# Encoder block on one core: two kinds of head pairs taken in turn, token loads first, statistics a block ahead

## The chip, the cores and the metric

The kernel runs on one core of one Trainium2 chip. The metric is the device time of one execution in microseconds. Three runs of the kernel before took 2289.86 to 2292.59 us, median 2290.41 us.

## The reference

One layer of a bidirectional encoder, run on two requests with the same weights: a prompt of 512 tokens and a sample of 1024 tokens, model width 1024.

```
h = rmsnorm(x);  proj = h @ w_in          # q, k, v of 8 heads A, q, k, v of 12 heads B, gates gA, gB
A: 2-D neighbourhood attention on rows of 64 tokens, window min(8, rows) x 16, bias rpb[head, dy, dx]
B: 3 groups of 4 heads, dilations 1, 4, 16; each query sees 64 keys on either side at its dilation,
   bias from a table of 32 buckets; the 3 groups are combined by their softmax denominators
merged = sigmoid(gA) * (oA @ wA) + sigmoid(gB) * (oB @ wB);   x = x + merged @ w_out
x = x + relu(rmsnorm(x) @ w_up)^2 @ w_down
```

All of it is float32 in the reference. q and k are normalised per head before the scores.

## The kernel before, in words

Both requests stand one behind the other as 1536 tokens, in three blocks b of 512 (block 0 is the prompt). Every large product is made of three fp16 matmuls on the high and low halves of both operands (`mm3`, lines 168 to 171); a weight is scaled by its own norm before it is halved.

**Stages.** First the tokens are normalised: `stats` (791) adds the squares of a block into `acc` and makes `rmsr`, the inverse norm of each token along the free axis, by way of two small matmuls (`ssx` 805, `bcx` 814) and a power on POOL (`rc` 810). `build` (782) multiplies the tokens by it (785, every third on POOL) and writes the halves `act` (hi 786 on ACT, lo 787 on DVE). Then come four gate column tiles g0 to g3 for the three blocks (`gate_mm`, 24 matmuls of 512 columns a block), then ten pairs of heads. Pairs 0 to 5 are dilated (B, two times the three dilations), pairs 6 to 9 are 2-D (A). A pair projects four token tiles of the prompt (names with `0b` or `0a`) and eight of the sample (`1b`, `1a`), 24 matmuls of 384 columns a tile (`pj0b`, `pj1a`...). One gate tile (g4 to g10) follows each of pairs 0 to 6, and five more (g11 to g15) follow pair 9. After that come the branch product, the output product and the MLP, from about 1015 us on.

**Attention** runs beside the projection of the pair behind it. `run` (680) advances by steps, a step being half a token tile of projection; the attention of a pair begins 8 steps after its last tile (LAG) and takes one unit every two steps: scores (`s`, `t`, 449), softmax, halves of the probabilities (`p`), a transposing DMA (`pT`, 470), and two units later the products with the values (`o`, 481 and 482). The normalised q and k are transposed by a DMA as well (`qk`, 382); v goes through memory (`v_d`, loaded as `v0b`, `v1a`...). A pairs load a bias of 256 KB (`ba0a`) or 768 KB (`ba1a`) three times a pair and a request; when the three groups of half of the B heads are done, `combine` (608) loads their outputs (`G`) and writes the combined ones. `branch_bound` (306) loads a weight in 18 pieces (`bn`) for its norm.

**Weights** (lines 71 to 122) stream through ten float32 slots (`st_g`, `st_p`) and fifteen fp16 slots (`w_g`, `w_p`). Each `tick` splits one piece, makes the scale of a tile that has all its squares (`scale_of`, with a small matmul `fro_g` or `fro_p`, 189, that stands in PE's queue), squares one piece and issues one load.

**Tables.** `tables` (688) builds the biases of both kinds in memory by DMAs from memory to memory: `vec_d`, `tb_d` (two of 768 KB), `tc_d` (two of 256 KB), 24 `r_d` of 30 KB, then `ct`, `c_d` and 21 pieces of `ba_d`. `b0b` and `b1b` load the B biases from them.

**What sets the order.** The program is written in the order that the Python code issues it, and buffers are recycled through pools; each engine works through its own queue in order. All DMAs but two are issued by SP, so the SP queue is one list in which a DMA that waits for its data holds every later one.

## Time and profile before

| | |
|---|---|
| median of 3 runs | 2290.41 us |
| the profiled execution's own time | 2283.75 us |
| its span, first to last instruction | 2282.0 us |
| mean granted clock of TensorE, of full speed | 0.976 |
| busy: PE, DVE, ACT, POOL | 2134.1, 1244.4, 993.5, 302.0 us |
| mean busy share of the 16 DMA engines, moved | 45% of the span for SP's queue, 259.10 MB |

PE is busy 94% of the span. The page's 40 slices (57 us each) show PE at 9 tenths or more in nearly all of them; the exceptions are the first four slices and those from the 12th to the 17th. The mean over the span says little about a stage, so the rows below cut it by stages: the start (0 to 96 us is blocks 0 and 1 of the gates, to 124 block 2), the B pairs from there to about 640, the A pairs to about 960, the last gates to 1040.

### The profile page before, as it was taken

The numbers are of one execution on the slowest core, as the hardware profiler recorded it, in microseconds if no ns is written. First come the engines' busy times: TensorE is split into PE (matmuls) and PEld (weight loads), VectorE is DVE, ScalarE is ACT, GpSimd is POOL, SyncE is SP. The second block draws the span as 40 slices with busy tenths as digits, with TensorE's granted clock in tenths as the row PEclk, the third lists the DMA queues.
The fourth block names the chain that finished last, engine by engine and source line by source line (L and its number), as shares of the span: only waits on it lengthen the run. The fifth ranks groups of instructions, "written<-read, shape, count | busy, mean of one in ns | idle before, by whom it ended". The sixth has DMA issues, their size and how long they took to land.

```text
span 2282.0 us, 32442 instructions
## 1 busy us (share of the span) xinstructions
PE 2134.1 (94%) x11440; PEld 1089.6 (48%) x11440; DVE 1244.4 (55%) x3245; ACT 993.5 (44%) x2432; POOL 302.0 (13%) x434
## 2 busy tenths in 40 slices
PE   5778999999997876989999999999999999999999
PEld 2334565556554544544444544444444444444444
DVE  6534766686567766646734544444444444444444
ACT  5234656566545664537633523233333333222222
POOL 1112322232223423100000000000000000000000
PEclk9888999999999998999999999999999999999999
DMA  5249886676669999878531110111111111111102
GB/s 165 77 140 264 196 178 156 156 175 144 142 135 188 189 186 184 173 177 283 191 130 37 56 32 28 52 56 56 56 56 56 56 56 56 39 38 36 37 1 111
DMA packets 372908, 259.10 MB, mean 114 GB/s; under 512 B 241152, under 2 KB 333184, under 8 KB 372744
## 3 DMA queue, kind: packets, MB, share of 16 engines
q1 hardware_dynamic: 372598, 257.01, 45.0%
q8 instruction: 90, 1.47, 0.3%
q14 instruction: 74, 0.61, 0.1%
q10 hardware_dynamic: 146, 0.01, 0.0%
HBM read 164.02 MB, written 53.29 MB: 95 GB/s over the span
## 4 chain that ended last, share of the span: by engine, by line
PE 71%; DMA 12%; DVE 5%; SPq 2%; ACT 2%; issue 1%; POOL 1%; ACTq 0%; DVEq 0%; POOLq 0%
PE up L169 7%; PE dn L169 7%; PE dn L170 7%; PE up L170 7%; PE dn L171 7%; PE up L171 7%; PE g L169 2%; PE g L170 2%; PE g L171 2%; PE pj1b L169 2%; PE pj1b L171 2%; PE pj1b L170 2%; PE op L169 2%; PE op L171 2%; PE op L170 2%; DMA pT1a<-p1a 2%
## 5 line engine op out<-in xcount | busy, mean ns | idle before, releaser
L948 DVE SCALAR_TENSOR_TENSOR y<-dn,und,y 128x512 f32<-128x512 f32 x384 | 287.0, 750 | 180.9 <-PE dn L171 180.6
L1126 ACT ACTIVATE r<-up,alpha 128x512 f32<-128x512 f32 x96 | 65.3, 680 | 592.2 <-PE up L171 592.1
L169 PE MATMUL up<-xp,w_u 128*128 128x512 f16 x768 | 291.0, 379 | 1.0 <-ACT xp L1049 1.0
L171 PE MATMUL dn<-w_d,u 128*128 128x512 f16 x768 | 291.1, 379 | 0.0
L171 PE MATMUL up<-xp,w_u 128*128 128x512 f16 x768 | 291.0, 379 | 0.0
L170 PE MATMUL dn<-w_d,u 128*128 128x512 f16 x768 | 291.0, 379 | 0.0
L170 PE MATMUL up<-xp,w_u 128*128 128x512 f16 x768 | 291.0, 379 | 0.0
L169 PE MATMUL dn<-w_d,u 128*128 128x512 f16 x768 | 291.0, 379 | 0.0
L1130 DVE TENSOR_TENSOR u<-r,u 128x512 f16<-128x512 f32 x96 | 66.3, 692 | 284.2 <-ACT u L1129 280.4
L169 PE MATMUL g<-act,w_g 128*128 128x512 f16 x384 | 148.3, 393 | 14.1 <-ACT act L786 14.1
L170 PE MATMUL g<-act,w_g 128*128 128x512 f16 x384 | 149.0, 388 | 6.1 <-DVE act L787 6.0
L171 PE MATMUL g<-act,w_g 128*128 128x512 f16 x384 | 148.8, 388 | 0.0
L169 PE MATMUL pj1b<-w_p,act 128*128 128x384 f16 x384 | 126.6, 330 | 2.4 <-DVE o1b L451 2.4
L171 PEld LDWEIGHTS <-act 128*128 128x128 f16 x960 | 95.6, 100 | 66.1 <-issue 6.9
L169 PEld LDWEIGHTS <-act 128*128 128x128 f16 x960 | 98.2, 102 | 60.0 <-issue 6.4
L170 PEld LDWEIGHTS <-act 128*128 128x128 f16 x960 | 96.5, 100 | 63.2 <-issue 11.3
L171 PE MATMUL pj1b<-w_p,act 128*128 128x384 f16 x384 | 126.1, 328 | 0.0
L170 PE MATMUL pj1b<-w_p,act 128*128 128x384 f16 x384 | 126.1, 328 | 0.0
L169 PEld LDWEIGHTS <-u 128*128 128x128 f16 x768 | 76.3, 99 | 89.0
L169 PEld LDWEIGHTS <-w_u 128*128 128x128 f16 x768 | 76.4, 100 | 88.5
L171 PEld LDWEIGHTS <-u 128*128 128x128 f16 x768 | 75.1, 98 | 90.6
L171 PEld LDWEIGHTS <-w_u 128*128 128x128 f16 x768 | 75.1, 98 | 90.5
(330 smaller groups left out, 4233.3 us busy)
## 6 DMA issues: line engine op xcount, KB each, us to landing
st_n<-in_wn SPq DMA_DIRECT2D x32, 512.0 KB
st_u<-in_wu SPq DMA_DIRECT2D x32, 512.0 KB
st_d<-in_wd SPq DMA_DIRECT2D x32, 512.0 KB
st_p<-in_wp SPq DMA_DIRECT2D x80, 192.0 KB
z_d<-z SPq DMA_DIRECT2D x48, 256.0 KB
z<-z_d SPq DMA_DIRECT2D x48, 256.0 KB
ba1a<-ba_d SPq DMA_DIRECT2D x12, 768.0 KB
st_g<-in_wg SPq DMA_DIRECT2D x32, 192.0 KB
```

Source lines behind the costliest of these rows:

```text
L169: nc.tensor.matmul(ps, ah, bh, start=first, stop=False)
L170: nc.tensor.matmul(ps, ah, bl, start=False, stop=False)
L171: nc.tensor.matmul(ps, al, bh, start=False, stop=last)
L948: nc.vector.scalar_tensor_tensor(out=out, in0=ps, scalar=scale, in1=out, op0=ALU.mult, op1=ALU.add)
L1126: nc.scalar.activation(s, ps[b], AF.Relu, scale=alpha[:, f:f + 1])
L1130: nc.vector.tensor_tensor(out=uu[:, 1, i, tb], in0=s, in1=uu[:, 0, i, tb], op=ALU.subtract)
```

## The change

1. ORDER and AFTER: the pairs are taken in the order B0 B1 B2 A6 B3 A7 B4 A8 B5 A9. Of the seven gate tiles between pairs, one stands behind pair 0 and two behind each of A6, A7 and A8. The first A pair waits until all tables have been issued, and the attention's generator doesn't end before the last combine.
2. `past`: a weight load is issued, and a piece squared early, by the count of splits of two ticks ago rather than the present one.
3. Start: tokens of block 0 are loaded ahead of most weights, those of blocks 1 and 2 right behind nine weight pieces. All squares of the tokens are made on ACT; their adds are made on DVE for block 0 and on POOL for blocks 1 and 2. The statistics of block b+1 are begun in the middle of block b, and three of its builds stand ahead of the fourth gate tile of block b. The steps of the tables begin in block 2.
4. The last steps of `ba_d` come every three steps of the background rather than every four.

```diff
+ORDER = (0, 1, 2, 6, 3, 7, 4, 8, 5, 9)
+AFTER = (1, 0, 0, 2, 0, 2, 0, 2, 0, 0)
...
-        while n and self.nload < min(len(self.units), self.nsplit + RAW):
+        while n and self.nload < min(len(self.units), self.past[0] + RAW):
...
-                                      or self.nload == self.nsplit + RAW):
+                                      or self.nload == self.past[0] + RAW):
...
+        self.past = [self.past[1], self.nsplit]
...
-    for i in range(10):
+    between, c = {}, NFIRST
+    for i, n in zip(ORDER, AFTER):
         W.add(("p", i), [(wp[i, k], 384) for k in range(KT)])
-        if i < NBETWEEN:
-            add_gate(NFIRST + i)
+        between[i] = range(c, c + n)
+        for c in between[i]:
+            add_gate(c)
+        c = between[i].stop
+    assert c == 16 - NFILL
...
-            for i, kind in enumerate(kinds):
+            for i in ORDER:
+                kind = kinds[i]
...
-                    if i < NBETWEEN:
-                        c = NFIRST + i
+                    for c in between[i]:
...
         def attn_a(self, p):
+            for _ in tab:
+                pass
...
+            while not self.combined:
+                yield
...
+            self.combined = True
...
-                for _ in range(4 if col else 2):
+                for _ in range(3 if col else 2):
...
-                src = xch[b][k]
-                if k == 0:
-                    nc.gpsimd.tensor_tensor(out=acc, in0=src, in1=src, op=ALU.mult)
-                else:
-                    sq = pp.tile([P, 512], F32, tag="p16", bufs=2, name=f"sqx{b}_{k}")
-                    nc.scalar.activation(sq, src, AF.Square)
-                    nc.vector.tensor_tensor(out=acc, in0=acc, in1=sq, op=ALU.add)
+                sq = pp.tile([P, 512], F32, tag="p16", bufs=2, name=f"sqx{b}_{k}") if k else acc
+                nc.scalar.activation(sq, xch[b][k], AF.Square)
+                if k:
+                    (nc.gpsimd if b else nc.vector).tensor_tensor(out=acc, in0=acc, in1=sq, op=ALU.add)
...
-            nc.gpsimd.tensor_tensor(out=rc, in0=rs, in1=mhalf, op=ALU.pow)
+            rsqrt(rc, rs)
...
         ld = load_x(0)
-        ps = [psum(f"g{c}_0") for c in range(3)]
-        W.load(3)
         for k in range(KT):
             next(ld)
-            if k % 2:
-                W.load(1)
+            if k == 3:
+                W.load(3)
+        W.load(6)
         gain()
         st = stats(0)
         next(st)
-        for _ in range(4):
-            W.tick(2)
-        next(st)
-        for _ in range(3):
-            W.tick(2)
-        next(st)
-        with tc.issue_after(xch["w"]):
-            for _ in load_x(1):
+        for b in (1, 2):
+            for _ in load_x(b):
                 pass
-        for k in range(KT):
-            build(0, k)
-            if k == 0:
-                W.ahead(("g", 2), 0)
-            for c in range(3):
-                gate_mm(c, 0, ps[c], k)
-        for c in range(3):
-            gate_out(c, 0, ps[c])
-        norms()
...
-        tab = tables(pp)
+        for _ in range(5):
+            W.tick(0)
         next(st)
         next(st)
-        for k in range(KT):
-            build(1, k)
+        norms()
+        tab = tables(pp)
+        ahead = 0
+        for b in range(NB):
+            ps = [psum(f"g{c}_{b}") for c in range(3)]
+            for k in range(KT):
+                if k >= ahead:
+                    build(b, k)
+                if b == 0 and k < 7:
+                    W.tick(0)
+                for c in range(3):
+                    gate_mm(c, b, ps[c], k)
+                if b == 2:
+                    next(tab)
+                if k == 4 and b < 2:
+                    st = stats(b + 1)
+                    next(st)
+            if b < 2:
+                next(st)
             for c in range(3):
-                if k == 0:
-                    ps[c] = psum(f"g{c}_1")
-                gate_mm(c, 1, ps[c], k)
-        for c in range(3):
-            gate_out(c, 1, ps[c])
-        st = stats(2)
-        next(st)
-        for c in range(3, NFIRST):
-            gate_step(c, 1)
-            next(tab)
-        next(st)
-        next(st)
-        for k in range(KT):
-            build(2, k)
-            for c in range(3):
-                if k == 0:
-                    ps[c] = psum(f"g{c}_2")
-                gate_mm(c, 2, ps[c], k)
-            next(tab, None)
-        for c in range(3):
-            gate_out(c, 2, ps[c])
+                gate_out(c, b, ps[c])
+            if b < 2:
+                next(st)
+                ahead = 3
+                for k in range(ahead):
+                    build(b + 1, k)
+            for c in range(3, NFIRST):
+                gate_step(c, b)
+                W.tick()
+                W.tick()
+        for c in range(NFIRST):
             W.release(("g", c))
             W.tick()
+            W.tick()
         tab = behind(tab)
-        for c in range(3, NFIRST):
-            gate_step(c, 2)
-            W.release(("g", c))
-            W.tick()
-            next(tab)
         at = Attention(pp)
         fill = gates(16 - NFILL, 16 - NLAST)
```

Three places show what this moves. The first is DVE's queue in the start, from the token norms to the first low halves (`rmsr` is the inverse norm, `w_g` a split gate weight, `xt` the tokens of block 0, `act` their halves, `acc` the sum of squares of block 1). Before:

```order
33 L817 COPY rmsr_261<-bcx_256 128x512
34 L258 SCALAR_TENSOR_TENSOR w_g_0_277<-st_g_0_144,scales,w_g_0_277 128x384
35 L190 TENSOR_REDUCE scales<-fro_g_294 128x1
36 L258 SCALAR_TENSOR_TENSOR w_g_1_284<-st_g_1_148,scales,w_g_1_284 128x384
37 L258 SCALAR_TENSOR_TENSOR w_g_2_291<-st_g_2_152,scales,w_g_2_291 128x256
38 L785 TENSOR_TENSOR xt_139<-xt_139,rmsr_261 128x512 x4
39 L785 TENSOR_TENSOR xt_6_140<-xt_6_140,rmsr_261 128x512
40 L785 TENSOR_TENSOR xt_7_141<-xt_7_141,rmsr_261 128x512
41 L801 TENSOR_TENSOR acc_450<-acc_450,sqx_5_464 128x512
42 L191 TENSOR_SCALAR scales<-scales 128x1
43 L787 SCALAR_TENSOR_TENSOR act_112<-xt_139,nvt,act_112 128x512 x4
```

And now:

```order
24 L827 COPY rmsr_256<-bcx_251 128x512
25 L798 TENSOR_TENSOR xt_130<-xt_130,rmsr_256 128x512 x4
26 L798 TENSOR_TENSOR xt_6_131<-xt_6_131,rmsr_256 128x512
27 L798 TENSOR_TENSOR xt_7_132<-xt_7_132,rmsr_256 128x512
28 L800 SCALAR_TENSOR_TENSOR act_112<-xt_130,nvt,act_112 128x512
29 L195 TENSOR_REDUCE scales<-fro_g_286 128x1
30 L800 SCALAR_TENSOR_TENSOR act_112<-xt_130,nvt,act_112 128x512 x3
```

The three weight splits and the add for block 1 (`acc_450`) no longer stand between the norms and the first low half.

The second place is the SP queue around the first tables (`tb_d`, `tc_d` tables of the B pairs, `st_g4_2` the last third of the weights of gate tile 4, `st_p1` pieces of pair 1, `b0b0` the bias of pair 0). Before:

```order
54 L711 DMA tb_d0_78<-vec_d_77 512x1x384
55 L707 DMA vec_d_77<-vec1_804 12x512
56 L707 DMA vec_d_77<-vec2_821 12x512
57 L711 DMA tb_d1_79<-vec_d_77 512x1x384
58 L547 DMA b0b0_1492<-tb_d0_78 128x2x384
59 L714 DMA tc_d0_80<-vec_d_77 512x1x128
60 L714 DMA tc_d1_81<-vec_d_77 512x1x128
61 L547 DMA b1b0_2136<-tb_d0_78 128x2x384
62 L232 DMA st_g4_2_924<-in_wg 128x256
63 L232 DMA st_p1_0_932<-in_wp 128x384
```

And now:

```order
48 L720 DMA vec_d_77<-vec0_819 12x512
49 L720 DMA vec_d_77<-vec1_836 12x512
50 L724 DMA tb_d0_78<-vec_d_77 512x1x384
51 L724 DMA tb_d1_79<-vec_d_77 512x1x384
52 L720 DMA vec_d_77<-vec2_853 12x512
53 L237 DMA st_g4_2_920<-in_wg 128x256
54 L237 DMA st_p1_0_925<-in_wp 128x384
55 L557 DMA b0b0_1483<-tb_d0_78 128x2x384
56 L237 DMA st_p1_1_930<-in_wp 128x384
57 L237 DMA st_p1_2_935<-in_wp 128x384
58 L237 DMA st_p1_3_942<-in_wp 128x384
59 L237 DMA st_p1_4_958<-in_wp 128x384
```

Both `tb_d` now stand together and ahead of `st_g4_2`, and `tc_d` has moved behind five pieces of pair 1. In PE's queue the `fro_g` of gate tile 4, for which `st_g4_2` is squared, has moved from within the first projected tile to ahead of it.

The third place is the SP queue in the prompt's attention of pair A6, between the transposes of its third and fourth units (`pT0a6_2`, `pT0a6_3`; `ba1a6` are the biases of the sample's units, `v1a6` its values, `st_p9` and `st_g11` weights, `o_d` outputs). Before, its last twelve rows:

```order
549 L232 DMA st_p9_2_8542<-in_wp 128x384
550 L232 DMA st_p9_3_8596<-in_wp 128x384
551 L532 DMA ba1a6_1_8940<-ba_d1_92 128x2x768
552 L232 DMA st_p9_4_8636<-in_wp 128x384
553 L232 DMA st_p9_5_8668<-in_wp 128x384
554 L232 DMA st_p9_6_8714<-in_wp 128x384
555 L232 DMA st_p9_7_8746<-in_wp 128x384
556 L502 DMA v1a6_2_8944<-v_d6_71 128x1x1024
557 L232 DMA st_g11_0_8807<-in_wg 128x384
558 L502 DMA v1a6_3_9340<-v_d6_71 128x1x1024
559 L527 DMA o_d_64<-o0a6_1_0_8598 16x8x128
560 L470 DMA_TRANSPOSE pT0a6_3_0_8564<-p0a6_3_0_8561 128x8x128
```

And now, with both transposes:

```order
335 L542 DMA ba1a6_0_5276<-ba_d0_91 128x2x768
336 L512 DMA v1a6_1_5469<-v_d6_71 128x1x1024
337 L478 DMA_TRANSPOSE pT0a6_2_0_4917<-p0a6_2_0_4914 128x8x128
338 L537 DMA o_d_64<-o0a6_0_0_4950 16x8x128
339 L542 DMA ba1a6_1_5467<-ba_d1_92 128x2x768
340 L651 DMA o_d_64<-G0_2_5219 128x2x128
341 L512 DMA v1a6_2_5471<-v_d6_71 128x1x1024
342 L478 DMA_TRANSPOSE pT0a6_3_0_5013<-p0a6_3_0_5010 128x8x128
```

Before, seven weight pieces stood among them. Now the weights are elsewhere and pair A6's prompt units begin beside two gate tiles, which need no transposes of q and k.

## Rows read from the trace of the kernel before

**Rows 1.** Windows: length, busy of PE, PEld, DVE, ACT, POOL, clock, DMA share, GB/s

```profile
0.00:20.00 20.00, 3.40 (x14) 3.21 (x14) 10.06 (x25) 13.53 (x36) 3.50 (x11) 1.00 0.84 269
58.00:96.00 38.00, 25.76 (x114) 12.05 (x114) 20.60 (x28) 11.75 (x19) 7.32 (x6) 0.85 0.24 86
96.00:124.00 28.00, 27.90 (x103) 10.21 (x102) 16.25 (x31) 7.41 (x13) 2.23 (x3) 0.83 0.19 65
107.50:115.50 8.00, 8.00 (x39) 3.62 (x38) 0.95 (x4) 0.00 (x0) 0.00 (x0) 1.00 0.28 100
124.00:202.00 78.00, 55.38 (x308) 31.57 (x305) 36.49 (x117) 34.35 (x106) 18.07 (x25) 0.84 0.75 203
202.00:640.00 438.00, 431.48 (x2798) 256.76 (x2799) 282.85 (x1089) 260.58 (x872) 119.35 (x165) 0.99 0.74 168
280.00:320.00 40.00, 40.00 (x261) 23.67 (x260) 23.44 (x82) 24.25 (x86) 8.48 (x12) 1.00 0.88 197
640.00:960.00 320.00, 260.73 (x1748) 153.58 (x1747) 222.92 (x841) 182.49 (x565) 97.41 (x140) 0.93 0.92 175
960.00:1040.00 80.00, 69.55 (x415) 35.67 (x413) 38.61 (x85) 35.56 (x69) 5.53 (x13) 0.94 0.85 218
```

**Rows 2.** Waits of PE, 0 to 220 us: total us, times, longest

```profile
PE fro_g L189 <- ACT wsq L239: 18.3, 2, 9.6
PE g L169 <- ACT act L786: 14.1, 3, 6.0
...
PE g L170 <- DVE act L787: 6.0, 2, 3.2
PE bcx L814 <- POOL rc L810: 3.5, 2, 2.0
```

**Rows 3.** Timeline of the start: start us, us, engine, instructions, idle time before

```profile
19.64 1.04 POOL L797 TENSOR_TENSOR acc<-xt 128x512 f32<-128x512 f32 x1 [8.01 <-DMA xt<-in_xt]
...
20.64 1.02 POOL L810 TENSOR_TENSOR rc<-rsx,mhalf 128x4 f32<-128x4 f32 x1
...
24.87 0.61 DVE L258 SCALAR_TENSOR_TENSOR w_g<-st_g,scales,w_g 128x384 f16<-128x384 f32 x1
...
25.47 2.95 DVE L258 SCALAR_TENSOR_TENSOR w_g<-st_g,scales,w_g 128x384 f16<-128x384 f32 x2
...
28.34 3.69 DVE L785 TENSOR_TENSOR xt<-xt,rmsr 128x512 f32<-128x512 f32 x6
...
34.07 0.59 PE L170 MATMUL g<-act,w_g 128*128 128x512 f16 x1 [3.23 <-DVE act L787]
```

**Rows 4.** Timeline of DVE at block 1's builds

```profile
61.28 5.83 DVE L785 TENSOR_TENSOR xt<-xt,rmsr 128x512 f32<-128x512 f32 x6
```

**Rows 5.** Timeline of the SP queue at the tables and behind them

```profile
105.92 0.70 SPq L711 DMA_DIRECT2D tb_d<-vec_d  x1
...
119.25 8.17 SPq L714 DMA_DIRECT2D tc_d<-vec_d  x2
...
130.44 0.47 SPq L232 DMA_DIRECT2D st_g<-in_wg  x1
```

**Rows 6.** Line 721, its issues on SP: min/median/max ns, first and last

```profile
L721 SPq DMA_DIRECT2D r_d<-in_rpb x24: 802/810/1577, 20.9 to 162.0; - x24
```

**Rows 7.** Line 470, transposes of the prompt's B units on SP

```profile
L470 SPq DMA_TRANSPOSE pT0b<-p0b x24: 1188/1192/2295, 196.8 to 612.3; - x24
```

**Rows 8.** Timeline of PE at the first product with values

```profile
202.12 0.29 PE L481 MATMUL o0b<-v0b,pT0b 64*128 64x128 f16 x1 [3.33 <-DMA pT0b<-p0b]
```

**Rows 9.** Waits of PE, 640 to 1050 us: total us, times, longest

```profile
PE o1a L481 <- DMA pT1a<-p1a: 27.4, 10, 6.9
PE o0a L481 <- DMA pT0a<-p0a: 22.7, 6, 7.4
PE o1a L481 <- DVE ss1a L364: 7.1, 2, 4.2
PE s1a L449 <- DVE mn1a L451: 5.8, 1, 5.8
```

More of the change, by code (lines that the diff above doesn't have):

```diff
@@ L76, in __init__ @@
         self.nload = self.nsq = self.nscale = self.nsplit = self.free = 0
+        self.past = [0, 0]
     def add(self, key, srcs):
@@ L269, in encoder @@
         add_gate(c)
-    NBETWEEN = 16 - NFIRST - NFILL
-    for i in range(10):
+    between, c = {}, NFIRST
+    for i, n in zip(ORDER, AFTER):
         W.add(("p", i), [(wp[i, k], 384) for k in range(KT)])
-        if i < NBETWEEN:
-            add_gate(NFIRST + i)
+        between[i] = range(c, c + n)
[3 more added lines that the diff above has]
+    assert c == 16 - NFILL
     for c in range(16 - NFILL, 16):
@@ L324, in __init__ @@
         def __init__(self, pp):
-            self.pp, self.step = pp, 0
+            self.pp, self.step, self.combined = pp, 0, False
             self.pairs = []
             kinds = [dict(kind="B", g=g, jj=jj) for jj in range(2) for g in range(NG)] + [dict(kind="A")] * 4
-            for i, kind in enumerate(kinds):
+            for i in ORDER:
+                kind = kinds[i]
                 for r in range(2):
@@ L767, in gain @@
         def gain():
-            row = pp.tile([1, D], F32, tag="p16", bufs=2, name="nvrow")
+            row = pp.tile([1, D], F32, tag="G", bufs=2, name="nvrow")
             nc.scalar.dma_start(out=row, in_=nvr)
@@ L862, in encoder @@
-        norms()
-        st = stats(1)
-        next(st)
-        for c in range(3, NFIRST):
-            gate_step(c, 0)
-        with tc.issue_after(xch["w"]):
-            for _ in load_x(2):
-                pass
-        tab = tables(pp)
+        for b in (1, 2):
+            for _ in load_x(b):
+                pass
+        for _ in range(5):
+            W.tick(0)
         next(st)
         next(st)
-        for k in range(KT):
-            build(1, k)
-            for c in range(3):
-                if k == 0:
-                    ps[c] = psum(f"g{c}_1")
-                gate_mm(c, 1, ps[c], k)
@@ L879, in encoder @@
-        for c in range(3):
-            gate_out(c, 1, ps[c])
-        st = stats(2)
-        next(st)
-        for c in range(3, NFIRST):
-            gate_step(c, 1)
-            next(tab)
-        next(st)
-        next(st)
-        for k in range(KT):
-            build(2, k)
-            for c in range(3):
-                if k == 0:
-                    ps[c] = psum(f"g{c}_2")
-                gate_mm(c, 2, ps[c], k)
-            next(tab, None)
-        for c in range(3):
-            gate_out(c, 2, ps[c])
+        norms()
@@ L897, in encoder @@
+        for c in range(NFIRST):
             W.release(("g", c))
             W.tick()
+            W.tick()
         tab = behind(tab)
-        for c in range(3, NFIRST):
-            gate_step(c, 2)
-            W.release(("g", c))
-            W.tick()
-            next(tab)
         at = Attention(pp)
@@ L908, in bounds @@
         def bounds():
-            while W.nscale < W.first["p", 9] + KT:
+            while W.nscale < W.first["p", ORDER[-1]] + KT:
                 yield
```

## The prediction

> **What bounds the kernel now.** I read the windows by stage first, then the waits of PE in the stages where it is not full, then the timeline and the SP queue at those places. PE has 2134.1 of 2282.0 us of work (the page), so a change of order can win only idle time and time at the low clock (half the full one: 1.2 of 2.4 GHz). The windows show where these lie [rows 1]. From 202 to 640 us, beside the B pairs, PE is busy 431.48 of 438 us at a clock of 0.99: nothing to win. From 640 to 960 us, beside the A pairs, it is busy 260.73 of 320 at 0.93. Before 202 us it is idle or slow in every stage. After 1040 us the change moves nothing. The reader should see two separate holes: about 59 us of idle time in the A stage and a bad first fifth of a millisecond.
>
> **Start, to the end of the first gates (now 124 us).** Three steps.
>
> First, the first low half reaches PE earlier. PE's first low matmul starts at 34.07 [rows 3]. (a) Block 0's tokens have six weight pieces among and ahead of them now and three in the new order: three pieces less, 512 KB, at 269 GB/s [rows 1] 1.9 us. (b) `rc` on POOL waits for the first square of block 1, 19.64 to 20.68, while its input is there at about 19.4: 1.2 us; in the new order nothing of block 1 is on POOL there. (c) Three weight splits stand on DVE from 24.87 until the first token product at 28.34: 3.5 us, gone. (d) One add for block 1, 0.7 us as its like, between the products and the low halves, and some 0.7 us of adds ahead of the copy of `rmsr`. Sum 8.0 us.
>
> Second, the waits at the borders of the blocks. PE waits for `act` high halves 14.1 us in three places (the longest, 6.0, at block 1), for low halves 6.0 in two (the longest, 3.2, at block 0) and for `rc` 3.5 in two [rows 2]. Block 0's own (5.8, 3.2, 2.0) belong to the first step. The rest is 14.1 - 5.8 + 6.0 - 3.2 + 3.5 - 2.0 = 12.6 us. With the statistics begun in the middle of the block before and three builds ahead of the fourth gate tile, ACT, DVE and POOL do this under 72 matmuls, 15 us at the 39 in 8.00 us of [rows 1]; I leave 1.4 us, since a high half now stands behind weight squares on ACT. Gain 11.2 us.
>
> Third, the clock. Behind those waits it was low: 0.85 of 38 us and 0.83 of 28 us [rows 1] cost at most 5.7 + 4.8 = 10.5 us; part of that time PE was idle anyway, so I take 7.5. The first gates end at 124 - 26.7 = 97.3 us.
>
> What pays for it: fourteen adds move to POOL. Six token products on DVE took 3.69 us with POOL idle and 5.83 us with POOL's products beside them [rows 3, 4], so 0.36 us for each DVE instruction beside one of POOL's. Fourteen of these are 5 us of DVE time under the 15 us above, twice: on the path 0, at most 5. The Trainium skill, "SBUF — State Buffer", section "Who interferes with whom", says that a DVE instruction with two SBUF inputs contends with a GpSimd instruction that reads SBUF, the port pair being held by one at a time. It speaks against this move, and the two rows agree in sign; by the rule the cost is bounded by the adds' own time, and the sum stays as it is as long as the cover holds.
>
> **From the first gates to the first product with values (now 202.12 [rows 8]).** Two waits of PE for squares of gate weights (`fro_g`) cost 18.3 us, 8.7 and 9.6 [rows 2]. The 9.6 goes: the gate tile behind pair 1 is gone, and the next scale of a gate is due behind pair A6. The 8.7 becomes about 5: the first `tb_d` went out at 105.92, 18 us ahead of the end of the gates [rows 5]; with the steps of the tables now in block 2 I put it at about 86, 11 us ahead. A `tb_d` takes 8 us (768 KB at 100 GB/s while it runs, with a DMA share of 0.28 [rows 1]: only some of the 16 engines work for it). Both run until 102, and `st_g4_2` stands behind them, where PE at 97.3 waits for it. This piece was issued at 130.44 [rows 5]; if it doesn't wait for `tb_d`, the 5 us are a gain too. The Trainium skill, "DMA: Bandwidth & Descriptors", section "Queues, rings and completion order", says that each DMA engine takes its descriptors in ring order; by it the small load waits for the table on the shared engines, and this speaks against the two tables in a row. Without it the sum would be 5 us lower.
>
> The clock from 124 to 202 is 0.84: 12.5 us at most [rows 1], in three stretches, one behind each wait; with one gone I count 5. Two small waits ahead of the first product (0.9, and 3.3 [rows 8]) are in the chain too. PE would then be at that place at 202.1 - 26.7 - 13.3 - 5 - 4.2 = 152.9.
>
> What is late next is the SP queue, which has to reach the first `pT0b`. From 102: `tc_d` 8.2 us [rows 5], some 4 us of weights and gates, then 24 `r_d` at 0.81 [rows 6], 20 us, all of which now stand ahead of or among the first transposes; 8 transposes of q and k at 1.2 [rows 7] to 1.7, about 11; 24 small issues at 0.5 (as the `st_g` [rows 5]), 12. Sum: 102 + 8 + 4 + 20 + 11 + 12 = 157 to 158, and from the issue to PE 5.3 us (196.8 [rows 7] to 202.1): PE goes on at about 163.5, having waited 10 us. Gain of the front 38 us. Its bounds: 49 if the queue is in time, 20 if the stretch from `tb_d` to `pT0b` stays as long as it is (196.8 - 105.9 = 90.9 us, from 86: 176.9, and 5.3). I take 38, since one wait on the queue of that stretch, the one for `st_g`, is gone.
>
> **The attention stages.** Idle now: 6.5 us beside the B pairs and 59.3 beside the A pairs, and 22.4 us at most of low clock there [rows 1]; 10.4 us of the tail are not touched. In the A stage PE waits for transposed probabilities: 22.7 us for the prompt's, 27.4 for the sample's, and 12.9 for DVE (`ss1a`, `mn1a`) [rows 9]. The cause is the SP queue: the transposes stand behind biases of 768 KB, values and weights, at a DMA share of 0.92, where the B stage has 0.74. The work is the same; only its neighbours change. Mixed, the share is (438 x 0.74 + 320 x 0.92) / 715, about 0.87, and at 0.88 PE ran 40.00 of 40 us [rows 1], so the mean alone doesn't force a wait. The prompt's units of A6, A7 and A8 fall into gate tiles, and the queue between two of their transposes loses its weights: of the 22.7 us I leave 5. The sample's units run beside B projections, whose q needs no copy to `qa` on DVE: of the 27.4, 6.9 are the last unit's and stay in the tail; of the other 20.5 I leave 10. Of the 12.9, 5; 6.5 stay beside the B pairs, and 3 come new from combining and from `bn` beside A6. So 30 of 65.8 us remain: 36 gained. Of the clock I count 17 as lost now and 7 then: 10. Sum 46, taken as 45. Bounds: 0 if the DMAs set the pace wherever they stand; 83 (65.8 and 17) if all goes.
>
> **Sum.** 2283.75 - 38 - 45 = 2200.75 on the profiled execution's scale. The median of the runs lies 6.7 us above that execution, so 2207 us.
>
> **Rivals.**
> - The A stage keeps its waits, because its DMAs need the time: 2283.75 - 38 + 6.7 = 2252. For it: a share of 0.92, and biases that stand ahead of transposes in the new queue too. Against it: 0.88 with no wait at all. Chance 0.15.
> - Nearly all waits go: 2283.75 - 49 - 83 + 6.7 = 2158. For it: the gate tiles as cover; against it: `pT` still behind 768 KB. Chance 0.10.
> - Both parts give only their lower bounds, 20 and 0 (the tables' queue stays as slow, and the mix doesn't help): 2270. Chance 0.07.
> - On the other side: the A pairs' DMAs stall the B pairs too. Their idle share, 59.3 of 320 = 18.5% [rows 1], then holds over the whole mixed stage of 758 us: 140 us instead of 66, and 2283.75 - 38 + 74 + 6.7 = 2326. It decides from 13.7% idle ((66 + 38) of 758). For it: one queue for all, and B's transposes behind A's biases; against it: the low end of the share's calculation. Chance 0.07.
>
> **Numbers.** Forecast 2207 with chance 0.61, its own range 2180 to 2235. To hold 8 in 10 I reach up over the first rival and down to 2170. About 0.2%, 4.6 us, is the least that runs of this kernel tell from none. Faster 0.91 (all but the last rival and a little of the third), same 0.02, slower 0.07.
>
> **What would show it.** First low matmul near 26 us; gates over near 97 us; a wait of about 5 us at `fro_g` ahead of the first projected tile; the first product with values near 163 us behind a wait of about 10 for `pT0b`; no wait over 2 us in the prompt's units of A6 to A8; idle time of PE from there to the last gates about 30 us. It is wrong if B units (`o1b`, `o0b`) wait in the mixed stage, or if the first product comes after 180 us.

## The result, and the profile after

The changed kernel takes 2253.53 us (median of 4 runs, 2251.05 to 2257.24) against 2290.14 us for the kernel before on the same chip: ratio 0.9849, 95% interval 0.9818 to 0.988. It is faster, as forecast, but the gain is 36.6 us and not 83; 2253.53 lies near the upper end of what was held with 8 in 10 (from 2170 to over the first rival's 2252) and outside the forecast's own range (2180 to 2235).

The profiled execution took 2257.24 us, span 2255.1; with 2283.75 and 2282.0 before, the traces differ by 26.9 us. (This execution lies 3.7 us above its median and the one of before 6.4 below, so the medians differ by more.) Where the 26.9 us are shows best in three stages cut at events that both traces have: the first product with values (`o0b`), the last pair's last projection (`pj1a`), the last product of attention (`o1a`). First the windows of before at these cuts: length, busy time of PE, PEld, DVE, ACT, POOL, granted clock, DMA share, GB/s.

```profile
0.00:202.12 202.12, 139.48 (x660) 71.11 (x661) 108.79 (x257) 87.44 (x219) 38.90 (x51) 0.89 0.51 152
202.12:925.59 723.47, 659.77 (x4344) 393.69 (x4344) 484.53 (x1863) 423.02 (x1380) 211.46 (x296) 0.96 0.81 171
925.59:1013.03 87.44, 78.08 (x507) 40.81 (x506) 44.44 (x128) 43.16 (x110) 9.88 (x20) 0.98 0.85 171
```

The same of the changed kernel:

```profile
0.00:188.80 188.80, 133.10 (x659) 69.72 (x659) 108.48 (x243) 87.13 (x223) 57.67 (x62) 0.93 0.53 156
188.80:882.33 693.53, 653.24 (x4369) 391.11 (x4370) 468.31 (x1762) 412.15 (x1364) 200.69 (x290) 0.98 0.83 177
882.33:983.99 101.66, 81.61 (x482) 40.92 (x480) 59.61 (x228) 44.34 (x126) 13.90 (x25) 0.91 0.71 169
```

The front gained 13.3 us (forecast 38) and the mixed stage 29.9 (45). The last gates lost 14.2, which the prediction held untouched, and what follows lost the remaining 2. PE's idle time is the length less its busy time: 62.6 to 55.7, 63.7 to 40.3, 9.4 to 20.0 us. What is left is clock: 0.89 to 0.93, 0.96 to 0.98, but 0.98 to 0.91 beside the last gates.

The start, by the timeline (start, us, engine, what, idle time before it), answering to [rows 3]:

```profile
18.14 2.61 POOL L811 TENSOR_TENSOR acc<-acc,sqx 128x512 f32<-128x512 f32 x2 [1.03 <-ACT sqx L809]
...
20.00 8.59 DVE L798 TENSOR_TENSOR xt<-xt,rmsr 128x512 f32<-128x512 f32 x6
...
29.31 0.58 PE L175 MATMUL g<-act,w_g 128*128 128x512 f16 x1 [6.40 <-DVE act L800]
```

The six token products begin at 20.00, where before they began at 28.34, but with POOL's adds and products beside them they take 8.59 us instead of 3.69. PE's first low half comes 4.8 us earlier, not 8.

PE's waits from 0 to 220 us (total us, times, longest), to be held against [rows 2] and [rows 8]:

```profile
PE o0b L489 <- DMA pT0b<-p0b: 14.3, 1, 14.3
...
PE g L175 <- DVE act L800: 7.6, 2, 6.4
PE fro_g L194 <- ACT wsq L244: 6.4, 2, 4.9
PE fro_p L194 <- ACT wsq L244: 5.4, 1, 5.4
PE g L174 <- ACT act L799: 3.6, 2, 2.9
```

`fro_g` fell from 18.3 to 6.4 us and the waits for high halves from 14.1 to 3.6. In their place stand a wait of 5.4 us for the squares of a projection and above all 14.3 us for the first transposed probabilities. The reason is on the SP queue (start, us, what; the time of a row holds its waits), which answers to [rows 5, 7]:

```profile
93.05 3.15 SPq L724 DMA_DIRECT2D tb_d<-vec_d  x2
96.28 7.64 SPq L720 DMA_DIRECT2D vec_d<-vec  x1
104.02 0.37 SPq L237 DMA_DIRECT2D st_g<-in_wg  x1
...
118.97 6.82 SPq L295 DMA_DIRECT2D z_d<-z  x4
...
128.23 3.51 SPq L734 DMA_DIRECT2D r_d<-in_rpb  x4
...
147.35 6.77 SPq L734 DMA_DIRECT2D r_d<-in_rpb  x8
...
171.79 5.04 SPq L391 DMA_TRANSPOSE qk1b<-q161b  x1
...
184.05 1.26 SPq L478 DMA_TRANSPOSE pT0b<-p0b  x1
```

From the first `tb_d` to the first `pT0b` 91.0 us pass; before, 90.9 [rows 5, 7]. The stretch moved forward as a whole and became no shorter. The second and third rows show another cost: `st_g4_2`, for which PE waits 4.9 us, went out only after the store of the third row of bias values (`vec_d`) had held the queue for 7.64 us. From its issue to its first reader on ACT another 7.5 us passed, while the two tables were in flight:

```profile
111.50 0.42 ACT L244 ACTIVATE wsq<-st_g 128x256 f32<-128x256 f32 x1 [13.18 <-DMA st_g<-in_wg]
```

In the mixed stage, from PE's waits of 188 to 985 us (the first row has both stages, 9.9 us of it ahead of the last gates):

```profile
PE o1a L489 <- DMA pT1a<-p1a: 19.5, 9, 6.7
...
PE o1b L489 <- DMA pT1b<-p1b: 8.2, 4, 3.2
...
PE o1b L489 <- DVE vst1b L361: 4.4, 1, 4.4
...
PE o0a L489 <- DMA pT0a<-p0a: 2.8, 1, 2.8
```

Beside the last gates, PE's waits from 882 to 985 us:

```profile
PE o1a L489 <- DMA pT1a<-p1a: 9.6, 2, 6.7
PE g L174 <- ACT z L184: 5.5, 2, 4.9
PE g L174 <- DVE z L186: 3.6, 2, 3.1
```

The two rows for `z`, the eviction of a gate's sum, are new. The timelines of DVE, ACT and PE show why:

```profile
918.60 0.17 DVE L630 TENSOR_TENSOR cm<-G 128x4 f32<-128x4 f32 x1 [7.29 <-DMA G<-g_d]
...
936.31 0.52 ACT L324 ACTIVATE bn<-bn 128x384 f32<-128x384 f32 x1 [5.66 <-DMA bn<-in_wb]
936.74 0.19 ACT L324 ACTIVATION_READ_ACCUMULATOR bn<-bn 128x1 f32 x1
936.83 0.67 ACT L184 ACTIVATE z<-g,ung 128x512 f32<-128x512 f32 x1
...
937.55 0.59 PE L174 MATMUL g<-act,w_g 128*128 128x512 f16 x1 [4.92 <-ACT z L184]
```

The square of `bn` waits 5.66 us for its load, the eviction stands right behind it on ACT, and PE's next gate matmul at 937.55 has waited 4.92 us for that eviction. On DVE the combining stands so (`cm` waits 7.29 us for `G` at 918.60): in the new order both pieces of background work fall beside the last gates.

### The profile page after: what moved, and what is told of

The parts are those of the page before. It is cut to its first block, busy times and chain, and to the rows that moved or that the text cites. A ratio compares the mean times of both kernels' runs of the same rounds, so it can differ in the third digit from the quotient of the medians.

```text
span 2255.1 us, 32452 instructions
## 1 busy us (share of the span) xinstructions
PE 2125.7 (94%) x11440; PEld 1086.0 (48%) x11440; DVE 1243.6 (55%) x3231; ACT 983.9 (44%) x2435; POOL 314.5 (14%) x445
## 4 chain that ended last, share of the span: by engine, by line
PE 70%; DMA 14%; DVE 7%; ACT 4%; issue 2%; SPq 2%; POOL 1%; POOLq 0%; ACTq 0%; DVEq 0%
PE up L174 7%; PE dn L174 7%; PE dn L176 7%; PE up L176 7%; PE up L175 7%; PE dn L175 7%; PE g L175 2%; PE g L174 2%; PE g L176 2%; PE op L174 2%; PE op L176 2%; PE op L175 2%; DMA qk0a<-q160a 1%; PE pj1b L174 1%; PE pj1b L176 1%
## 5 line engine op out<-in xcount | busy, mean ns | idle before, releaser
L174 PE MATMUL g<-act,w_g 128*128 128x512 f16 x384 | 149.2, 392 | 13.3 <-ACT z L184 5.5
```

The source lines that it names most:

```text
L174: nc.tensor.matmul(ps, ah, bh, start=first, stop=False)
```

## The experiments

All are edits of the changed kernel, shown cut; each median is followed by its ratio to the kernel before on the same chip, with the 95% interval. The runs come from several chips, on which the kernel before takes 2283.87 to 2290.14 us, so versions are compared by these ratios; the changed kernel has 0.9849 (0.9818 to 0.988). Stages are cut at the same events as above, each in one profiled execution.

**The two halves of the change apart.** The first run has the new start with the old order of heads, the second the new order with the old start.

```diff
-ORDER = (0, 1, 2, 6, 3, 7, 4, 8, 5, 9)
-AFTER = (1, 0, 0, 2, 0, 2, 0, 2, 0, 0)
+ORDER = (0, 1, 2, 3, 4, 5, 6, 7, 8, 9)
+AFTER = (1, 1, 1, 1, 1, 1, 1, 0, 0, 0)
```

> Start, statistics and load rule of the changed kernel, but the pairs in the old order with one gate tile behind each of pairs 0 to 6. If the two halves of the change add up, this gives the front's share alone: the first product with values came 13.3 us earlier (202.1 to 188.8), so about 2277 us against 2290, with the A stage waiting as before (about 59 us idle between 640 and 960). Rival, the order of the gate tiles matters in the front too: the wait of 9.6 us for the squares of gate tile 5 comes back, the first product with values is near 198 us and the time 2285 to 2290.

2272.23 us, 0.9935 (0.992 to 0.9949). The first product with values comes at 193.1, the mixed stage takes 718.0, the last gates 90.3. The wait for gate tile 5 came back, as the rival had it and longer, and still the front gained 9.0 us; another 5.5 come in the mixed stage, which neither expectation has.

```diff
-        while n and self.nload < min(len(self.units), self.past[0] + RAW):
+        while n and self.nload < min(len(self.units), self.nsplit + RAW):
...
-                (nc.gpsimd if b else nc.vector).tensor_tensor(out=acc, in0=acc, in1=sq, op=ALU.add)
+                    nc.vector.tensor_tensor(out=acc, in0=acc, in1=sq, op=ALU.add)
...
-            if k == 3:
-                W.load(3)
-        W.load(6)
+            if k % 2:
+                W.load(1)
```

> The new order of pairs and gate tiles in the kernel before, with its old start, statistics and load rule. If the halves add up: 16 us from the attention stage, about 2274 us, first product with values still near 200 us. Rival, the order gives the whole gain, front included, since the gate tile behind pair 1 is gone: first product with values 10 us earlier and about 2260 us.

2277.22 us, 0.9954 (0.9938 to 0.9971); first product at 202.3, mixed stage 701.1, last gates 101.7. The loss beside the last gates thus belongs to the order alone. In the front each half is held by what the other takes away: with the new start alone, PE waits 15.94 us at `fro_g` (to 165.69), the gate tile behind pair 1 being still there; with the order alone, one `fro_g` wait is gone and the transposes take all of it:

```profile
PE o0b L487 <- DMA pT0b<-p0b: 12.0, 1, 12.0
PE fro_g L192 <- ACT wsq L242: 9.2, 1, 9.2
```

By the ratios the halves give 0.65% and 0.46%, together 1.51%; the 0.4% between them is within what the intervals leave open.

**POOL's adds back on DVE.**

```diff
-                    (nc.gpsimd if b else nc.vector).tensor_tensor(out=acc, in0=acc, in1=sq, op=ALU.add)
+                    nc.vector.tensor_tensor(out=acc, in0=acc, in1=sq, op=ALU.add)
```

> The changed kernel with the fourteen adds for blocks 1 and 2 back on DVE. Port theory (POOL's adds slow DVE's token products beside them: six took 8.59 us, 3.69 before): the six take about 4 us plus any adds between them, the first low matmul comes near 25 us instead of 29.3, the gates end 5 us earlier and the whole kernel gains 5 us against the changed one (2248). Rival, DVE's own time: fourteen adds of 0.69 us on DVE cost the same 5 us elsewhere in block 0, and the time stays at 2253 within 2 us.

2254.8 us, 0.9858 (0.9842 to 0.9873): not told apart from the changed kernel, as the rival had it. DVE's six products at the start, from the timeline:

```profile
20.83 5.83 DVE L798 TENSOR_TENSOR xt<-xt,rmsr 128x512 f32<-128x512 f32 x6
```

So POOL's adds cost these six 2.8 us. PE's first low half comes at 27.98, the first product with values at 185.8, 3 us earlier; the runs show none of it.

**The 24 `r_d` issues: ahead of the stretch, and twice.** The first kernel issues them at the border of blocks 0 and 1 (52.7 to 73.5 us); the second issues each a second time into a tensor that nobody reads.

```diff
+    def rows():
+        for ci, j in enumerate((0, 1, 3)):
...
+                nc.sync.dma_start(out=r_d[ci][16 * h:16 * h + 16].rearrange("c r k -> r c k"), in_=src)
...
+            if b == 0:
+                with tc.issue_after(xch["w"]):
+                    rows()
```

> The changed kernel with the 24 r_d issues moved from behind the tables of the B pairs to the border of blocks 0 and 1, where SP is idle. Queue theory (the first transposed probabilities are late because SP has 91 us of issues and waits between tb_d and pT0b): that stretch shrinks by the 20 us of r_d to 71 to 75 us, the wait of 14.3 us for pT0b falls to about 1, the waits of 2.4 and 1.3 us ahead of it go too, the first product with values comes near 173 us and the kernel gains 13 to 16 us against the changed one (2238 to 2240). Rival, the queue waits for the producers of q, k and v and not for itself: gain under 4 us, pT0b still near 180 us.

2247.34 us, 0.9822 (0.9805 to 0.9838). The first product with values, in the timeline of PE:

```profile
175.91 0.28 PE L489 MATMUL o0b<-v0b,pT0b 64*128 64x128 f16 x1 [7.47 <-ACT q161b L386]
```

```diff
+                q.dma_start(out=r_x[ci][16 * h:16 * h + 16].rearrange("c r k -> r c k"), in_=src)
```

> The changed kernel with each of the 24 r_d issues doubled, the copies into a scratch that nobody reads: 24 issues of 0.81 us, 20 us, more on SP ahead of the first pT0b. Queue theory: the stretch from tb_d to pT0b grows from 91 to about 110 us, the first product with values comes near 207 us instead of 188.8, and the kernel loses 12 to 20 us (2265 to 2273). Rival, SP mostly waits for producers in that stretch and hides the issues: under 4 us.

2275.08 us, 0.996 (0.9946 to 0.9973):

```profile
208.93 0.28 PE L490 MATMUL o0b<-v0b,pT0b 64*128 64x128 f16 x1 [15.04 <-DMA pT0b<-p0b]
```

The first product comes 12.9 us earlier without them and 20.1 later with twice as many; their own time in the changed kernel is 24 x 0.80 = 19.3 us. Added issues between `tb_d` and `pT0b` are on the path in full. Taken off, they shorten the stretch to 79.7 us (`pT0b` at 172.80), and PE then waits 7.47 us for a half of q and k made on ACT (`q161b`) and not for the queue. So the queue is what ended last in the changed kernel, with another limit close behind it. Over the whole kernel the early issues give less than was expected: 0.27% by the ratios, with intervals that overlap, and 9.7 us between the two profiled spans. Twice the issues cost 1.1%, clear of the intervals.

**Tables, and the rows they are built from (`vec_d`), on ACT's queue.** The `r_d` issues stand early here too.

```diff
-            q.dma_start(out=tb_d[g], in_=bass.AP(src.tensor, src.offset + g * VEC + 128, [[NG * VEC, HG], [-1, P], [1, 384]]))
+            nc.scalar.dma_start(out=tb_d[g], in_=bass.AP(src.tensor, src.offset + g * VEC + 128, [[NG * VEC, HG], [-1, P], [1, 384]]))
```

> The kernel with the early r_d, and vec_d, tb_d and tc_d (the tables of the B pairs) issued by ACT instead of SP. Queue theory: SP is held 7.6 us by the last vec_d, which waits for DVE, and by the pieces behind the tables; freed of them st_g4_2 is issued near 93 us instead of 104, the waits of 4.9 us at fro_g and 5.0 at fro_p go, and pT0b is issued 12 to 15 us earlier: first product with values near 162 us instead of 175.9, 10 to 14 us gained against the kernel with the early r_d (2234 to 2237). Rival, the DMA rings: the loads wait on the engines that the tables occupy, whichever queue issues them: st_g4_2 still lands near 110 us and the gain is under 3 us.

2245.44 us, 0.9825 (0.9809 to 0.9841), which is no better than the early `r_d` alone. The third `vec_d` now held ACT's queue (96.14 to 103.84), weight splits on ACT came late and `st_g4_2` was issued at 105.18; PE waited 9.09 us at `fro_g` and not at `fro_p`. Whether `st_g4_2` waits for the tables on the DMA engines or only for its turn on the queue, this run doesn't tell, as ACT squares the piece only at 115.42; other traces bear on it (`fro_g` in the next section).

**Tables a block earlier.** Their one-hot rows get buffers that are free by then, and the steps run from block 1 on; with that the `r_d` issues move ahead too, to 25 to 57 us.

```diff
-            ohs.append(pp.tile([33, VEC], F32, tag="pT", bufs=NPT, name=f"oh{g}"))
+            ohs.append(pp.tile([33, VEC], F32, tag="G", bufs=2, name=f"oh{g}"))
...
-                if b == 2:
+                if b:
```

> The changed kernel with the steps of the tables begun in block 1 instead of block 2 (the one-hot rows take the buffers of G, which are free there): vec_d, tb_d, tc_d and r_d are then issued before 90 us. Queue theory: no table stands between the gates and the first transposes, the waits of 4.9 and 5.4 us for weight squares shrink to under 2 each, pT0b is issued by 155 us, and the first product with values comes near 158 to 162 us instead of 188.8; some of it is given back at the first transposes of pair 0's sample, as 3 of 13 us were with the early r_d: 18 to 24 us gained against the changed one (2230 to 2236). Rival, the first attention waits for its own producers (q and k through ACT, POOL and DVE): not before 172 us, as with the early r_d, and under 10 us gained.

2235.54 us, 0.9787 (0.977 to 0.9803). The gain over the changed kernel is clear, that over the early `r_d` alone just so. `tb_d` goes out at 69.7, both waits for weight squares are gone and `pT0b` costs 2.2 us; the first product comes at 173.5, later than the 158 to 162 expected. New waits came up at the border of blocks 1 and 2:

```profile
PE g L175 <- DVE act L800: 15.0, 4, 8.1
PE g L174 <- ACT act L799: 5.8, 2, 3.0
PE bcx L824 <- POOL rc L189: 5.0, 1, 5.0
```

ACT stood 16.17 us in front of an eviction of `z` whose buffer was still being stored by a DMA, with the next block's high halves behind it.

**Gates one by one instead of two behind each 2-D pair.**

```diff
-AFTER = (1, 0, 0, 2, 0, 2, 0, 2, 0, 0)
+AFTER = (1, 0, 0, 1, 1, 1, 1, 1, 1, 0)
```

> The changed kernel with the six gate tiles one behind each of pairs A6, B3, A7, B4, A8 and B5 instead of two behind each of A6, A7 and A8. If gate tiles are what covers the prompt's units of the A pairs: waits for pT0a rise from 2.9 us towards half of the 22.7 us of before, and the kernel loses 8 to 12 us. Rival, taking the kinds in turn does it: waits for pT0a stay under 5 us and the time within 3 us.

2278.27 us, 0.9965 (0.9951 to 0.9978). The mixed stage takes 719.1 us (the old order with the new start: 718.0), and PE's waits from 180 to 910 us have the prompt's transposes back, 22.7 us before [rows 9] and 2.8 in the changed kernel:

```profile
PE o0a L489 <- DMA pT0a<-p0a: 17.5, 5, 6.4
```

The rival is out, and the loss is more than twice the 8 to 12 us expected: by this run, taking the pairs in turn gives nothing by itself, and the 25 us that the mixed stage gains hang on two gate tiles behind each 2-D pair. 14.7 of them are the waits for `pT0a`.

**The weights' look-back.** Here a weight's buffer is taken again as soon as its last split is issued, as before.

```diff
-        while n and self.nload < min(len(self.units), self.past[0] + RAW):
+        while n and self.nload < min(len(self.units), self.nsplit + RAW):
```

> The changed kernel with the old load rule (a load is issued as soon as the count of splits allows). If the rule matters: SP waits for the split of a slot again, 25 us in the first 220 us as in the kernel before, and the kernel loses 5 to 10 us. Rival, SP is held by tables and gates anyway: no change within 3 us.

2261.86 us, 0.9898 (0.9878 to 0.9918), with a span 3.7 us longer; the front is the same (188.6), the mixed stage takes 697.1. On SP the wait for splits of gate weights is 10.2 us in the first 220, against 9.4 in the changed kernel, and not the 25 expected. By the ratios the rule is worth 0.5%, some 11 us, but the intervals overlap by a hair, so it may be worth next to nothing.

**Branch bound early.** `bn` is loaded and squared in the last sample pair's first half and no longer behind the combining.

```diff
+            while not at.half:
+                yield
+            yield from branch_bound(pp)
...
-            yield from branch_bound(pp)
```

> The changed kernel with the 18 loads and squares of branch_bound begun when the first half of the B heads is combined, not when pair 9 has its scales. Theory of the last gates: evictions of gate tiles stand on ACT behind squares that wait for bn, and on DVE behind the combine that waits for G; without bn there the wait of 4.9 us (ACT z) goes and that of 3.1 us (DVE z) stays, with its low clock some 6 us gained (2247). Rival, the combine alone holds both: the waits for z stay at 8 to 9 us and the time at 2253.

2253.68 us, 0.9865 (0.9848 to 0.9883): no difference by the runs, where 6 us were expected. In its profile the wait for ACT's `z` is gone and the last gates take 96.1 us instead of 101.7:

```profile
PE o1a L489 <- DMA pT1a<-p1a: 7.4, 2, 6.7
PE g L174 <- DVE z L186: 6.5, 2, 4.1
```

**The last dilated pair ahead of the last but one 2-D pair,** so that both combinings are over before the last gates.

```diff
-ORDER = (0, 1, 2, 6, 3, 7, 4, 8, 5, 9)
-AFTER = (1, 0, 0, 2, 0, 2, 0, 2, 0, 0)
+ORDER = (0, 1, 2, 6, 3, 7, 4, 5, 8, 9)
+AFTER = (1, 0, 0, 2, 0, 2, 0, 0, 2, 0)
```

> The changed kernel with pair B5 ahead of A8 (B0 B1 B2 A6 B3 A7 B4 B5 A8 A9) and the last two gate tiles between behind A8, so that the second combine falls beside A8 and A9 and not beside the last gates. If that combine (with branch_bound) holds the evictions of the last gates: their stretch shrinks from 101.7 to about 88 us, the mixed stage loses 2 to 4 us by having two A pairs in a row, and the kernel gains 8 to 12 us against the changed one. Rival, pair A9's own units hold them: the stretch stays over 98 us and the time within 3 us.

2260.8 us, 0.9871 (0.9852 to 0.989). No wait for `z` is left and the last gates take 92.0 us, 9.7 less. But two 2-D pairs now follow each other, and the mixed stage takes 708.7, 15 more; PE's waits over both stages:

```profile
PE o1a L489 <- DMA pT1a<-p1a: 24.8, 13, 6.7
...
PE o0a L489 <- DMA pT0a<-p0a: 12.7, 3, 8.7
```

`bn` still stands beside the last gates here, so most of the loss there comes from the place of the combining (with the last dilated pair), as supposed; the order that avoids it costs 15 us elsewhere where 2 to 4 were expected, and the kernel is not faster.

**Putting it together.** Early tables and early `bn` in one kernel:

> The early tables and, with them, the 18 loads of branch_bound begun when the first half of the B heads is combined. If the two add up: the early tables' time less 3 to 5 us, 2226 to 2232. Rival, what the tail gives is taken by bn loads beside pair A6: the same as the early tables alone.

2227.94 us, 0.9758 (0.9741 to 0.9776): first product at 171.2, mixed stage 684.0, last gates 98.0. That is the time expected, but by the intervals it is not told apart from the early tables alone. Then four more edits: the first gates' stores on ACT's queue, the rows of bias values in a buffer of their own, the `ct` steps of the tables three steps later, the last dilated pair ahead as above.

```diff
-        nc.sync.dma_start(out=z_d[c, :, b * 512:b * 512 + 512], in_=z)
+        (nc.scalar if c < NFIRST else nc.sync).dma_start(out=z_d[c, :, b * 512:b * 512 + 512], in_=z)
...
+        vecs = pp.tile([12, NG, VEC], F32, tag="qk0", bufs=2, name="vecs")
...
-            vs = pp.tile([12, VEC], F32, tag="p16", bufs=2, name=f"vec{g}")
+            vs = vecs[:, g]
```

> The kernel with early tables and early bn, and in it: this order with B5 ahead of A8, the vec rows in a buffer of their own kind (qk0, free at the start), the ct steps three later, and the evictions of the first four gate tiles sent by ACT's queue instead of SP's. If the waits at the border of blocks 1 and 2 there (4.1, 2.5 and 8.6 us) come from evictions queued behind tb_d and from a memset on POOL that waits for a vec: they fall under 2 us in all, the first product with values comes near 159 us instead of 171, and with the last gates the time is 2204 to 2214. Rival, DVE and POOL have too much to do there: the waits stay over 10 us and only the tail gains, 2218 to 2224.

2224.36 us, 0.9718 (0.9703 to 0.9732). Its windows:

```profile
0.00:158.78 158.78, 128.31 (x646) 67.93 (x647) 99.74 (x220) 80.97 (x204) 52.78 (x57) 0.98 0.65 200
158.78:863.59 704.81, 654.59 (x4359) 391.41 (x4360) 488.63 (x1883) 421.51 (x1404) 215.29 (x302) 0.98 0.83 174
863.59:948.87 85.28, 77.77 (x507) 40.64 (x504) 46.38 (x133) 42.30 (x106) 9.77 (x20) 0.98 0.85 171
```

With these edits the front ends at 158.8, ahead of the 163.5 forecast for the change, and the last gates are back at 85.3. The mixed stage gives 21 us back (with the last dilated pair moved alone it lost 15), so the time falls into the rival's range. The last run keeps all of this but the order of the changed kernel:

> The start of the version before this (tables from block 1 on, their rows in a buffer of their own, the first gates' stores of z on ACT's queue, branch bound early) with the changed kernel's own order of heads instead of B5 ahead of A8. Theory 1: the stages are separate, so the gains add: first product with values at 159 us as in the version before, then 684 us of mixed stage and 98 of last gates as in the run with early tables and early branch bound alone, 1267 for the rest: a profiled span near 2208 us and a median near 2212, ratio about 0.967. Theory 2: the mixed stage is bound by the queue wherever it starts, so an earlier start only makes it longer: the mixed stage 697 to 700 us and the median near 2224, ratio about 0.972, no gain from the order.

2219.82 us (2217.27 to 2227.46), 0.97 (0.9676 to 0.9723), the fastest median; by the intervals not told apart from the run before. Its windows (the profiled execution took 2227.46, 7.6 above the median):

```profile
0.00:159.06 159.06, 127.18 (x647) 67.84 (x647) 100.16 (x220) 81.27 (x204) 52.78 (x57) 0.98 0.66 199
159.06:858.43 699.37, 657.00 (x4383) 392.85 (x4384) 477.01 (x1791) 422.37 (x1398) 204.66 (x297) 0.98 0.84 174
858.43:956.14 97.71, 81.69 (x483) 40.75 (x481) 57.79 (x226) 41.79 (x111) 12.54 (x25) 0.92 0.77 165
```

The front's 12 us are won here too. In this profile the mixed stage takes 699.4 us instead of 684.0, but the profile is of the slowest of the five runs. By the ratios, 0.9758 and 0.97, with intervals that don't overlap, this kernel is 0.6%, some 13 us, faster than the early tables with early `bn`: over the runs the front's 12 us arrive. The time lies between the two theories (2212 and 2224) and decides for neither. Why this one execution has a longer mixed stage is open: the waits for transposes are the same in both profiles (16.9, 8.0 and 5.8 us against 17.5, 8.0 and 6.4), and the rest is spread over waits of 1 to 4 us for DVE and ACT.

## Why the prediction was right in sign and wrong in size

- **The step that failed:** "What is late next is the SP queue", with the first `pT0b` at 157 to 158. It came at 184.05. The bound stood beside it ("20 if the stretch from `tb_d` to `pT0b` stays as long as it is"), and the stretch did stay as long. The start of its `r_d` issues was put at 114 and came at 128.2: 7 us of this since the first `tb_d` went out at 93.05 and not at 86 (blocks 1 and 2 were slower than thought), 7 since stores wait on SP for what they store (`vec_d` 7.64 us, and four `z_d` 6.82 us from 118.97). From there to `pT0b` 43.5 us were counted and 55.8 measured: the 24 `r_d` took 21.0 us (20 counted), the 8 transposes of q and k 15.4 (11; one alone 5.04, waiting for its half), the small issues, 29 and not 24, and the gaps between them 19.4 (12). Together 26.5 us, against the 25.3 by which the first product was late. The prediction summed the queue's issue times and left its waits out; the trace lists 25.8 us of them in the new stretch. One reason it gave for the shorter value, the wait for `st_g` gone, weighs nothing: weight loads wait 4.0 us for splits in the old stretch and 2.0 in the new, where 3.7 for a table's DMA come to it. And 8 of the 24 `r_d` issues stood ahead of the stretch before and all 24 stand in it now, 8 x 0.80 = 6.4 us more; that about as much went out of it elsewhere, so that 90.9 and 91.0 agree so closely, is chance. That the issues are on the path is shown by the two `r_d` runs; the shares of the waits are read from the trace alone.
- **PE's own path, the "152.9", was wrong as well.** PE stood ready for the first product at 188.80 - 14.33 = 174.5, 21.6 us late: 9.9 from the first gates (below), and 9.1 in three waits that were not foreseen, 5.4 at `fro_p`, 2.4 for `qn1b` and 1.3 for `vst1b`; the rest is not traced. So with the queue in time the gain of the front would not have been 49: with the early `r_d` PE was ready at 168.4 and waited for ACT.
- **The first gates** were forecast to end at 97.3 and ended at 107.2. All three terms were too large. The first low half came 4.8 us earlier and not 8.0: the products began 8.3 us earlier, about as counted, and then took 8.59 us instead of 3.69. "On the path 0, at most 5" for POOL's adds had no place for this: with the adds on DVE the six take 5.83, so the adds cost them 2.8 us, and POOL's two products, which before had ended when DVE's began, the other 2.1. The sentence of the Trainium skill on the shared port ("SBUF — State Buffer", "Who interferes with whom") had the sign, and that run agrees. Taken out, the adds give 3 us in the profile and nothing in the runs. From the first low half to the end of the gates PE's idle time fell from 12.5 to 4.0 us (1.4 forecast), and its busy time, where the clock shows, from 77.4 to 73.9: 3.5 us and not the 7.5 taken, though the granted clock rose from 0.89 to 0.98.
- **`fro_g`**: 18.3 to 6.4 us, with 4.9 ahead of the first projection (forecast 5). The size was right, and the traces speak for the reason, a load that waits for two tables, with all of it some 10 us later than forecast. From its issue to its first reader the piece took 7.5 us, and 7.5 and 7.6 with the early `r_d` and with the new start alone, where both tables are in flight too; with the tables a block earlier it took 2.3 (110.67 to 112.96). That is as the Trainium skill's rule on ring order has it ("DMA: Bandwidth & Descriptors", "Queues, rings and completion order"). No run isolates it: in the first three the store of `vec_d` held the queue until 104 as well.
- **The mixed stage**: the prompt's `pT0a` waits fell from 22.7 to 2.8 us (forecast 5), the sample's `pT1a` outside the last gates from 18.1 to 9.9 (forecast 10; the longest of before, 6.9, was not the last unit's, as the prediction had it, that one is 6.7). The mechanism was right, and the gates one by one show it from the other side. Mis-sized were the waits for DVE ("Of the 12.9, 5"): over this stage they sum to 19.0 us before and 18.7 after. The B units' waits were left as they were, but those for `pT1b` rose from 3.4 to 8.2; with that for `vst1b` on DVE (4.4) they are what the prediction named as a sign of being wrong, as was a first product after 180. Idle time fell by 23.4 us in this stage where 36 were forecast, busy time by 6.5 where the clock was to give 10.
- **The last gates**: "10.4 us of the tail are not touched" and "3 come new from combining and from `bn` beside A6". The order puts the second combining and `bn` beside the last gates and not beside A6; ACT and DVE hold the evictions of gates behind a DMA wait, PE idles 10.6 us more and its granted clock there falls from 0.98 to 0.91. Cost 14.2 us. The run with the new order alone has the same 14.3, and with the last dilated pair moved 9.7 of them go.
- **The rivals**: the measured time, 2253.5, is that of the first rival (2252), but not for its reason. The prompt's waits in the 2-D units did go and half of the sample's; it was the front and the last gates that didn't give. That the number agrees is luck. The rival with all DMAs pulling the B pairs down (2326) didn't come: DMA share 0.83, clock 0.98, 40 us idle.

## What to carry to other kernels

When a chain of work moves earlier as a whole, measure its length in the trace from first issue to last, waits included, and keep that length unless a wait inside it is shown to go; the sum of issue times is a lower bound and no forecast. When work is reordered, list what lands beside every later stage, above all instructions that wait for a DMA on an engine that also evicts for TensorE. And stage times of one profiled execution are not the runs: in the last version the profile shows none of the 13 us of gain that the runs show.

## What the runs showed of the hardware

- Six VectorE products of 128x512 fp32 take 3.69 us with POOL idle, 5.83 beside POOL's products, 8.59 beside its products and adds; POOL's adds took 1265 to 1717 ns each in the changed kernel.
- One issue of a 15x16x32 table on SP takes 0.80 us and a small weight piece 0.33 to 0.58: the 24 table issues are 19.3 us of queue time that no DMA share shows (the share of the front is 0.53).
- A weight piece of 128 KB reached its reader 7.5 to 7.6 us after its issue in three kernels that had two tables of 768 KB in flight, and 2.3 us after it where the second of them had been issued 30 us earlier. That it waits for the tables is what the times suggest; no run isolates it.
- A store stands on its queue until its source is written. `vec_d` held SP for 7.64 us with `st_g4_2` behind it, and moved to ACT's queue it held ACT for 7.7.
